# The head of a pooling and state-space decoder step, written in another order

## The chip, the cores and the metric

The kernel runs on one core of a Trainium2 chip. The metric is the device time of one launch in microseconds (us): the median over repeated runs. One further execution is recorded by the hardware profiler. Its span runs from the first instruction to the last; its own time is a little longer. A core has a matrix engine (TensorE, PE in the profile, with PEld for its weight loads), VectorE (DVE), ScalarE (ACT), GpSimd (POOL) and SyncE (SP), which here only issues transfers (DMA).

## The reference

One layer of a decoder, on a prompt of 1,024 rows and on 64 sample rows (8 sequences of 8), model width 1,024. Cut to what the change touches:

```python
mod = jax.nn.silu(c) @ w_ada + b_ada
shift, scale, gate = jnp.split(mod, 3, axis=-1)
h = rmsnorm(x, norm_g) * (1 + scale[:, None]) + shift[:, None]
proj = h @ w_in
u_pool, z_pool, z_ssm, xbc, dt_raw, g_raw = jnp.split(proj, SPLITS, axis=-1)
...
dt = jax.nn.softplus(dt_raw.astype(jnp.float32) + dt_bias.astype(jnp.float32))
...
y = (y + d_skip.astype(jnp.float32)[:, None] * xs).reshape(b, L, D_INNER)
...
gates = jax.nn.sigmoid(g_raw)
m = gates[..., :D_MODEL] * p + gates[..., D_MODEL:] * s
x = x + gate[:, None] * (m @ w_o)
```

Everything behind `proj` (pooling, convolution, the state-space scan, the output projections, the final norm) follows the head and is the same in both kernels.

## The kernel before

All 1,088 rows are kept transposed: a tile has 128 channels on the partitions and 1,088 rows along its free axis, and the model width makes eight such tiles, numbered k. Matrix products in float32 are made from a high and a low part: a matrix is split into `whi` (ACT rounds it) and `wlo` (the rest, by GpSimd or DVE), and the other operand likewise, so each product is three matmuls.

The head is `first()` (L775 to L911) with the lines ahead of it (L127 to L149). It calls `in_line` (L295) at its beginning and end: every instruction that it issues on PE, ACT, DVE, GpSimd and SP keeps the order in which the Python code writes it, engine by engine. Behind the head a scheduler chooses the order. So an instruction that waits holds up all that is written behind it on its engine, and the change is a change of these written orders.

The stages of the head, as written before:

1. `c` (nine rows: one of the prompt, eight of the samples) is loaded into `c9`, ACT takes its silu (L137), PE turns it (transposes it by a matmul with the identity, L142) and DVE copies the result to `scT` (L143). Small vectors in `vb` (among them b_ada and the norm gains) are turned into `vT` (L146 to L148).
2. The rows of x, nine tiles of up to 128 rows: `x_square` (sum of squares, DVE or ACT), `x_root` (ACT), `x_unit` (DVE: reciprocal and scaling in place).
3. `x_turn(g, k)` (L210) turns three groups of rows (x0 and x1; x2 to x4; x5 to x8) for each of the eight k into the tiles `tf[k]`; PE writes a PSUM bank, ACT (odd k) or DVE (even k) copies it out.
4. `ada_mm(part, k)` (L235) multiplies scT by w_ada, eight steps of four matmuls for each of the two parts; `ada_end(part)` (L242) turns the result and adds the bias into `md`. Part 0 serves k = 0 to 3, part 1 serves k = 4 to 7.
5. `h_make(block, ks)` (L264) makes h = tf x scale + shift in high and low parts on ACT and DVE for a block of rows (256, 384 or 448).
6. `products(block, ks)` (L793) multiplies h with two tiles of w_in columns (those of the first gates), six PSUM banks that are filled over k = 0 to 7. `done(block, t)` (L810) takes the sigmoid on ACT and stores it.
7. `late_loads` (L327): its first step issues loads, its second (`next(late)`) copies d_skip into `dx` on DVE (L337), turns `va` (L339) and `dx` (L340) on PE and copies them to `cvT` and `Dv` (L341, L342).
8. `dt_block` (L673): the 32 columns of dt, 32 matmuls for each block.
9. The first pair of column tiles is multiplied by a scheme with seven products instead of eight (`strassen`, L556, with `early=True`). `pair_w.first_steps` (L499) makes its seven split weights from b11, b12, b21 and b22: its first step splits b11 and b21 and forms three differences, later steps split the others. `combine()` (L435) makes the sums S2, S3 and S1 of the tf tiles in place on DVE, ACT copies the high part (L441), DVE makes the low part (L442). The seven products run in `run(wz, hook)`; `hook` interleaves further sums and weight steps.

The low parts and the DVE operations of step 9 share DVE; ACT holds one set of function tables at a time, and each change of set (square root, silu, sigmoid) is an ACT_TABLE_LOAD.

Of the kernel before, what the change touches and what calls it, by code (L numbers as in the profile page):

```python
# [8 lines left out]
F32 = mybir.dt.float32  # L9
F32R = mybir.dt.float32r  # L10
AF = mybir.ActivationFunctionType
ALU = mybir.AluOpType
# [8 lines left out]
P = 128  # L21
D = 1024
KT = D // P
# [23 lines left out]
def tile_pool_ssd_step(  # L47
# [6 lines left out]
    nc = tc.nc  # L54
# [41 lines left out]
    def PB():  # L96
        return psB.tile([P, 512], F32, tag="ps", name=nm("ps"))
# [10 lines left out]
    act = nc.scalar.activation  # L108
    V = nc.vector
# [14 lines left out]
        nc.gpsimd.memset(rc[:, t:t + 1], 1.0 / (t + 1))  # L124


    act(rc[:, 0:1], eps, AF.Silu)  # L127
    nc.gpsimd.memset(rc[:, 0:1], 1.0)
    c9 = R([NB + 1, D])
    store_(c9[0:1, :], c_prompt)  # L130
    store_(c9[1:NB + 1, :], c_sample)
# [2 lines left out]
    store_(vb[16:24, :], norm_g[0].rearrange("(m p) -> m p", p=P))  # L134
    store_(vb[24:40, :], ssm_norm_g[0].rearrange("(m p) -> m p", p=P))
    store_(vb[40:44, :], pool_scale[0].rearrange("(m p) -> m p", p=P))
    act(c9, c9, AF.Silu)  # L137
    scT = const([P, KT, 32], "scT")
    nc.gpsimd.memset(scT, 0.0)
    ps = PB()  # L140
    for k in range(KT):
        nc.tensor.transpose(ps[:, k * 9:k * 9 + 9], c9[:, k * P:(k + 1) * P], ident[:9, :9])  # L142
    V.tensor_copy(scT[:, :, 0:9], ps[:, :72].rearrange("p (k b) -> p k b", b=9))  # L143
    vT = const([P, 44], "vT")
    ps = PB()
    nc.tensor.transpose(ps[:, :44], vb, ident[:44, :44])  # L146
    V.tensor_copy(vT, ps[:, :44])
    V.tensor_scalar(vT[:, 8:16], vT[:, 8:16], 1.0, None, ALU.add)  # L148
    pscl = vT[:, 40:44]  # L149


    def split(raw, kept=None, ncols=P, eng=None):
# [37 lines left out]
    def x_square(i, eng):  # L190
        xt, n = xr[i]
        sqj = pa.tile([P, D], F32, tag="rawA", name=nm("sqj"), bufs=3)
        if eng is V:
            V.scalar_tensor_tensor(sqj[:n], xt[:n], 1.0, xt[:n], ALU.mult, ALU.mult, accum_out=ss[:n, i:i + 1])
        else:
            act(sqj[:n], xt[:n], AF.Square, accum_out=ss[:n, i:i + 1])

    def x_root(a, b):
        n = xr[a][1]
        act(rs[:n, a:b], ss[:n, a:b], AF.Sqrt, bias=eps[:n], scale=1.0 / D)  # L200
# [6 lines left out]

    tf = [None] * KT

    def x_turn(g3, k):  # L210
        if g3 == 0:
            tf[k] = tfp.tile([P, T], F32, tag="tf", name=nm("tf"), bufs=8)
        px = PB()
        c = 0
        for i in range((0, *XG)[g3], XG[g3]):
            xt, n = xr[i]
            nc.tensor.transpose(px[:, c:c + n], xt[:n, k * P:(k + 1) * P], ident[:n, :n])
            c += n
        o = BLK[g3][0]
        if k % 2:  # L220
            act(tf[k][:, o:o + c], px[:, :c], AF.Copy)
        else:
            V.tensor_copy(tf[k][:, o:o + c], px[:, :c])
# [211 lines left out]
    def combine():  # L435
        L_, R_ = slice(0, HF), slice(HF, T)

        big = []

        def parts(src, hi, lo):  # L440
            act(hi, src, AF.Copy)  # L441
            V.tensor_tensor(lo, src, hi.bitcast(F32), ALU.subtract)  # L442

        def part(lst, k, src):
            if lst is S1:
                lst[k] = (hs.tile([P, 2, HF], F32R, tag="sq", name="S1", bufs=1) if k == 3 else R((P, 2, HF), F32R))
            else:
                if k == 0:
                    big.append(Y4(hs).rearrange("p k (j n) -> p k j n", j=2))
                lst[k] = big[-1][:, k]  # L450
            parts(src, lst[k][:, 0], lst[k][:, 1])
        for k in range(4):
            a, b = tf[k], tf[k + 4]
            V.tensor_tensor(b[:, R_], a[:, R_], b[:, R_], ALU.add)
            V.tensor_tensor(a[:, R_], a[:, L_], a[:, R_], ALU.subtract)
            V.tensor_tensor(a[:, L_], b[:, R_], a[:, L_], ALU.subtract)
            part(S2, k, a[:, L_])
            yield
        for k in range(4):
            part(S3, k, tf[k][:, R_])  # L460
        yield
        for k in range(4):
            a, b = tf[k], tf[k + 4]
            V.tensor_tensor(b[:, L_], b[:, L_], a[:, L_], ALU.subtract)
            part(S1, k, b[:, R_])
            if k % 2:
                yield
        for k in range(4):
            parts(tf[k + 4][:, L_], hh_[k][:, R_], hl_[k][:, R_])
            if k % 2:  # L470
                yield
# [303 lines left out]
    def first():  # L775
        ET = mybir.EngineType
        every = (ET.PE, ET.Activation, ET.DVE, ET.Pool, ET.SP)
        in_line(every, True)
        raws = {}

        def w_load(t, j):
            raws[t, j] = raw_()
            c = C_G + D + t * P
            load(raws[t, j], w_in[0, j * 512:(j + 1) * 512, c:c + P].rearrange("(k p) c -> p k c", p=P))

        w = {}

        def w_split(t, j, eng=None):
            w[t, j] = split(raws[t, j], eng=eng)

        banks = {}

        def products(bi, ks):  # L793
            o, n = BLK[bi]
            for t in range(2):
                if (bi, t) not in banks:
                    banks[bi, t] = (PB if (bi, t) in ((1, 1), (2, 0), (2, 1)) else PA)()[:, :n]
            for k in ks:
                for t in range(2):
                    ps = banks[bi, t]  # L800
                    hi, lo = w[t, k // 4]
                    a, b = hi[:, k % 4, :], lo[:, k % 4, :]
                    rh, rl = hh_[k][:, o:o + n], hl_[k][:, o:o + n]
                    mm(ps, a, rh, start=(k == 0), stop=False)
                    mm(ps, b, rh, start=False, stop=False)
                    mm(ps, a, rl, start=False, stop=(k == KT - 1))

        tags = iter(("s1", "u2", "u3", "c2", "s1", "u2"))

        def done(bi, t):  # L810
            o, n = BLK[bi]
            buf = pa.tile([P, HF], F32, tag=next(tags), name=nm("g0"))
            act(buf[:, :n], banks[bi, t], AF.Sigmoid)
            store_(gs_d[t][:, o:o + n], buf[:, :n])

        for i in range(9):
            x_load(i)
        for k in range(KT):
            if k == KT - 2:
                w_load(0, 0)  # L820
                w_load(1, 0)
            ada_load(0, k)
        for k in range(KT):
            if k == 2:
                w_load(0, 1)
                w_load(1, 1)
            ada_load(1, k)
        late = late_loads()
        next(late)

        x_square(0, V)
        x_square(1, V)
        x_root(0, 2)
        x_square(2, None)
        x_unit(0, 2)
        x_square(3, V)
        x_root(2, 4)
        x_square(4, None)
        x_root(4, 5)
        x_unit(2, 4)  # L840
        for k in range(8):
            x_turn(0, k)
        x_unit(4, 5)
        x_square(5, None)
        x_square(7, V)
        x_square(6, None)
        ada_mm(0, 0)
        for k in range(4):
            x_turn(1, k)
        x_root(5, 8)  # L850
        x_unit(5, 8)
        ada_mm(0, 1)
        x_square(8, None)
        x_root(8, 9)
        for k in range(4, 8):
            x_turn(1, k)
        x_unit(8, 9)
        ada_mm(0, 2)
        ada_mm(0, 3)
        for k in range(4):  # L860
            x_turn(2, k)
        ada_mm(0, 4)
        for k in range(4, 8):
            x_turn(2, k)
        ada_mm(0, 5)
        w_split(0, 0)
        w_split(1, 0)
        ada_mm(0, 6)
        ada_mm(0, 7)
        ada_end(0)  # L870

        h_make(0, range(4))
        products(0, range(4))
        h_make(1, range(4))
        ada_mm(1, 0)
        ada_mm(1, 1)
        w_split(0, 1, V)
        w_split(1, 1, V)
        products(1, range(4))
        h_make(2, range(4))  # L880
        for k in range(2, 8):
            ada_mm(1, k)
        products(2, range(2))
        ada_end(1)
        dtw = dt_w()
        products(2, range(2, 4))

        for bi in range(3):
            h_make(bi, range(4, 8))
        next(late, None)  # L890
        for bi in range(3):
            products(bi, range(4, 8))
            for t in range(2):
                done(bi, t)

        run, (wz, wst) = light[0][1], light[0][0]()
        next(wst)
        sums = combine()
        for i in range(3):
            next(sums)  # L900
            dt_block(dtw, i)
        next(sums)
        next(wst)

        def hook(n):
            if 0 < n < 4:
                next(wst)
            if n < 5:
                next(sums)
        run(wz, hook)  # L910
        in_line(every)  # L911
# [950 lines left out]
```

## Time and profile before

| | us |
|---|---|
| median of 3 runs | 1326.1 |
| lowest and highest run | 1325.13, 1326.57 |
| the profiled execution's own time | 1323.45 |
| its span | 1321.4 |
| PE busy in the span | 1264.8 (96%) |
| DVE, ACT, POOL busy | 890.4, 697.6, 679.5 |

A row of a timeline gives start, duration, engine, line, operation, tile written <- tiles read, shapes, count; the bracket tells how long the engine was idle before it and what released it. A row of the stretches gives the length, then busy us and instructions of each engine, the clock granted to PE (1.00 is full), the busy share of the DMA engines and GB/s.

### The profile page before, as it was taken

The numbers are of one execution on the slowest core, as the hardware profiler recorded it, in microseconds if no ns is written. First come the engines' busy times: TensorE is split into PE (matmuls) and PEld (weight loads), VectorE is DVE, ScalarE is ACT, GpSimd is POOL, SyncE is SP. The second block draws the span as 40 slices with busy tenths as digits, with TensorE's granted clock in tenths as the row PEclk, the third lists the DMA queues.
The fourth block names the chain that finished last, engine by engine and source line by source line (L and its number), as shares of the span: only waits on it lengthen the run. The fifth ranks groups of instructions, "written<-read, shape, count | busy, mean of one in ns | idle before, by whom it ended". The sixth has DMA issues, their size and how long they took to land.

```text
span 1321.4 us, 26075 instructions
## 1 busy us (share of the span) xinstructions
PE 1264.8 (96%) x9575; PEld 1164.8 (88%) x9575; DVE 890.4 (67%) x1510; ACT 697.6 (53%) x1661; POOL 679.5 (51%) x564
## 2 busy tenths in 40 slices
PE   5588999999999999999999999999999999999998
PEld 3468989999999999999889999988888888999786
DVE  5647557997967997877657665387565877567433
ACT  4725445656656655555554563667887767201211
POOL 0002666887887787764444453366676646314000
PEclk9898999999999999999999999999999999999999
DMA  9425644554554564543556555999988665475621
GB/s 320 146 68 178 211 167 143 172 178 139 195 192 153 164 188 132 165 149 113 158 143 196 176 159 171 341 346 369 311 268 284 193 202 157 163 262 167 218 100 60
DMA packets 232568, 251.66 MB, mean 190 GB/s; under 512 B 31101, under 2 KB 173573, under 8 KB 232434
## 3 DMA queue, kind: packets, MB, share of 16 engines
q1 hardware_dynamic: 160308, 171.56, 40.9%
q10 hardware_dynamic: 72134, 78.45, 17.4%
q8 instruction: 76, 1.25, 0.4%
q14 instruction: 50, 0.41, 0.1%
HBM read 167.06 MB, written 83.01 MB: 189 GB/s over the span
## 4 chain that ended last, share of the span: by engine, by line
PE 70%; DMA 10%; issue 7%; DVE 5%; POOL 4%; ACT 3%; ACTq 0%; SPq 0%; POOLq 0%; DVEq 0%
PE ps L550 7%; PE mm L550 7%; PE ps L551 7%; PE ps L552 7%; PE mm L552 7%; PE mm L551 7%; PE mm L315 3%; PE mm L316 3%; PE mm L317 3%; PE ps L1810 2%; PE ps L1809 2%; PE ps L1808 2%; PE ps L1134 2%; PE ps L1350 1%; POOL G L1717 1%
## 5 line engine op out<-in xcount | busy, mean ns | idle before, releaser
L158 POOL TENSOR_TENSOR wlo<-rawA,whi 128x512 fp32r<-128x512 f32 x120 | 193.3, 1616 | 198.6 <-ACT whi L155 110.6
L158 POOL TENSOR_TENSOR wlo<-raw,whi 128x512 fp32r<-128x512 f32 x92 | 150.7, 1645 | 131.7 <-ACT whi L155 125.2
L315 PE MATMUL mm<-Y,whi 128*128 128x352 f32 (+1 forms) x480 | 164.8, 343 | 0.8 <-DVE G L1711 0.6
L316 PE MATMUL mm<-Y,whi 128*128 128x352 f32 (+1 forms) x480 | 158.6, 330 | 1.0 <-DVE Y L1385 1.0
L317 PE MATMUL mm<-Y,wlo 128*128 128x352 f32 (+1 forms) x480 | 158.2, 330 | 0.0
L550 PE MATMUL mm<-Y,whi 128*128 128x272 f32 x496 | 146.8, 296 | 1.5 <-ACT dts L683 1.2
L552 PE MATMUL mm<-Y,wlo 128*128 128x272 f32 x496 | 143.1, 289 | 2.5 <-POOL wlo L158 2.5
L550 PE MATMUL ps<-Y,whi 128*128 128x272 f32 x496 | 144.5, 291 | 0.4 <-ACT s L593 0.4
L551 PE MATMUL mm<-Y,whi 128*128 128x272 f32 x496 | 143.2, 289 | 0.4 <-DVE Y L442 0.4
L551 PE MATMUL ps<-Y,whi 128*128 128x272 f32 x496 | 143.1, 289 | 0.0
L552 PE MATMUL ps<-Y,wlo 128*128 128x272 f32 x496 | 142.8, 288 | 0.0
L155 ACT ACTIVATE whi<-rawA 128x512 fp32r<-128x512 f32 x125 | 78.2, 626 | 104.4 <-PE ps L551 46.5
L942 DVE SCALAR_TENSOR_TENSOR GA<-GA,cvT,GA 128x1112 f32<-128x1112 f32 x72 | 130.1, 1812 | 0.0
L155 ACT ACTIVATE whi<-raw 128x512 fp32r<-128x512 f32 x96 | 58.7, 626 | 87.2 <-DVE raw L497 51.5
L550 PEld LDWEIGHTS mm<-Y,whi 128*128 128x128 f32 x496 | 93.4, 188 | 5.9 <-ACT dts L683 2.0
L315 PEld LDWEIGHTS mm<-Y,whi 128*128 128x128 f32 x480 | 91.3, 190 | 6.9 <-issue 4.1
L552 PEld LDWEIGHTS mm<-Y,wlo 128*128 128x128 f32 x496 | 93.4, 188 | 3.5 <-POOL wlo L158 3.2
L550 PEld LDWEIGHTS ps<-Y,whi 128*128 128x128 f32 x496 | 93.3, 188 | 3.4 <-issue 2.7
L551 PEld LDWEIGHTS mm<-Y,whi 128*128 128x128 f32 x496 | 93.4, 188 | 1.5 <-DVE Y L442 0.8
L551 PEld LDWEIGHTS ps<-Y,whi 128*128 128x128 f32 x496 | 93.3, 188 | 0.3 <-issue 0.2
L552 PEld LDWEIGHTS ps<-Y,wlo 128*128 128x128 f32 x496 | 93.4, 188 | 0.2 <-issue 0.2
L316 PEld LDWEIGHTS mm<-Y,whi 128*128 128x128 f32 x480 | 91.4, 190 | 1.7 <-DVE Y L1385 1.6
(446 smaller groups left out, 3784.3 us busy)
## 6 DMA issues: line engine op xcount, KB each, us to landing
rawA<-in_w_in SPq DMA_DIRECT2D x46, 512.0 KB
dec<-acs_d SPq DMA_DIRECT2D x32, 512.0 KB
xbc<-GA ACTq DMA_DIRECT2D x24, 512.0 KB
xb<-xbc SPq DMA_DIRECT2D x32, 384.0 KB
rawA<-in_w_in SPq DMA_DIRECT2D x32, 256.0 KB
pw<-in_w_ssm_out ACTq DMA_DIRECT2D x32, 256.0 KB
ws<-ph ACTq DMA_DIRECT2D x32, 256.0 KB
ws<-pw SPq DMA_DIRECT2D x32, 256.0 KB
```

The lines of the kernel that those rows point to most:

```text
L155: ins = act(hi[:, :, :ncols], raw[:, :, :ncols], AF.Copy)
L158: (eng or nc.gpsimd).tensor_tensor(lo[:, :, :ncols], raw[:, :, :ncols], hi[:, :, :ncols].bitcast(F32), ALU.subtract)
L315: mm(ps[:, :n], a, rh[k][:, o:o + n], start=(k == 0), stop=False)
L316: mm(ps[:, :n], a, rl[k][:, o:o + n], start=False, stop=False)
L317: mm(ps[:, :n], b, rh[k][:, o:o + n], start=False, stop=(k == nk - 1))
L550: mm(p, hi, ah, start=(k == 0), stop=False)
L551: mm(p, hi, al, start=False, stop=False)
L552: mm(p, lo, ah, start=False, stop=(k == 3))
L942: V.scalar_tensor_tensor(d[:, :n], rp[:, k:k + n], cvT[:, 24 * k + mc:24 * k + mc + 1], d[:, :n], ALU.mult, ALU.add)
L1134: mm(o[hh], xd[:S, 2 * q + hh, :], dec[:S, 2 * q + hh], start=True, stop=state is None)
L1808: mm(ps[:, :cw], mhk, wo[k][0][:, s], start=(k == 0), stop=False)
L1809: mm(ps[:, :cw], mhk, wo[k][1][:, s], start=False, stop=False)
```

## The change

The written order of the head is rearranged; the operations are the same apart from the engine of one square and two copies.

- The silu of `c` moves from the start into the turning of the third row group (`c_turn`), and so does the turning of `vb` (`v_turn`). ACT's first table load is that of the square root.
- The roots and scalings of x stand earlier, one square moves from DVE to ACT, and the first four turnings are all copied by DVE. The ada steps of part 0 stand together behind the third group's first four turnings; the turnings (2, 5) to (2, 7) stand behind the first `h_make`.
- In `combine`, the low part of each S2 tile is written behind the next tile's sums.
- `next(late)` moves from ahead of the second half's products to behind the last sigmoids and the first sums. The next pair's first weight step (`next(wst)`) moves ahead of the sigmoids, the first sums ahead of the last two sigmoids.

```diff
-    act(rc[:, 0:1], eps, AF.Silu)
-    nc.gpsimd.memset(rc[:, 0:1], 1.0)
...
-    act(c9, c9, AF.Silu)
+
+    act(rc[:, 0:1], eps, AF.Sqrt)
+    nc.gpsimd.memset(rc[:, 0:1], 1.0)
...
+    def c_turn():
+        act(c9, c9, AF.Silu)
+        ps = PB()
+        for k in range(KT):
+            nc.tensor.transpose(ps[:, k * 9:k * 9 + 9], c9[:, k * P:(k + 1) * P], ident[:9, :9])
+        V.tensor_copy(scT[:, :, 0:9], ps[:, :72].rearrange("p (k b) -> p k b", b=9))
+
+    def v_turn():
+        ps = PB()
+        nc.tensor.transpose(ps[:, :44], vb, ident[:44, :44])
+        V.tensor_copy(vT, ps[:, :44])
+        V.tensor_scalar(vT[:, 8:16], vT[:, 8:16], 1.0, None, ALU.add)
...
+        def low(k):
+            V.tensor_tensor(S2[k][:, 1], tf[k][:, L_], S2[k][:, 0].bitcast(F32), ALU.subtract)
         for k in range(4):
             a, b = tf[k], tf[k + 4]
+            room(S2, k)
             V.tensor_tensor(b[:, R_], a[:, R_], b[:, R_], ALU.add)
             V.tensor_tensor(a[:, R_], a[:, L_], a[:, R_], ALU.subtract)
             V.tensor_tensor(a[:, L_], b[:, R_], a[:, L_], ALU.subtract)
-            part(S2, k, a[:, L_])
-            yield
+            act(S2[k][:, 0], a[:, L_], AF.Copy)
+            if k:
+                low(k - 1)
+            if k < 3:
+                yield
+        low(3)
+        yield
...
         x_root(0, 2)
+        x_unit(0, 2)
         x_square(2, None)
-        x_unit(0, 2)
-        x_square(3, V)
+        x_square(3, None)
         x_root(2, 4)
+        for k in range(4):
+            x_turn(0, k, V)
+        x_unit(2, 4)
         x_square(4, None)
         x_root(4, 5)
-        x_unit(2, 4)
-        for k in range(8):
+        for k in range(4, 8):
             x_turn(0, k)
         x_unit(4, 5)
         x_square(5, None)
         x_square(7, V)
         x_square(6, None)
-        ada_mm(0, 0)
+        x_root(5, 8)
         for k in range(4):
             x_turn(1, k)
-        x_root(5, 8)
         x_unit(5, 8)
-        ada_mm(0, 1)
         x_square(8, None)
         x_root(8, 9)
         for k in range(4, 8):
             x_turn(1, k)
         x_unit(8, 9)
-        ada_mm(0, 2)
-        ada_mm(0, 3)
+        v_turn()
+        for k in range(2):
+            x_turn(2, k)
+        c_turn()
+        for k in range(2, 4):
+            x_turn(2, k)
         for k in range(4):
-            x_turn(2, k)
-        ada_mm(0, 4)
-        for k in range(4, 8):
-            x_turn(2, k)
-        ada_mm(0, 5)
+            ada_mm(0, k)
         w_split(0, 0)
         w_split(1, 0)
-        ada_mm(0, 6)
-        ada_mm(0, 7)
+        for k in range(4, 8):
+            ada_mm(0, k)
+        x_turn(2, 4)
         ada_end(0)
 
         h_make(0, range(4))
+        for k in range(5, 8):
+            x_turn(2, k)
         products(0, range(4))
...
-        next(late, None)
         for bi in range(3):
             products(bi, range(4, 8))
+
+        run, (wz, wst) = light[0][1], light[0][0]()
+        next(wst)
+        for bi in range(2):
             for t in range(2):
                 done(bi, t)
-
-        run, (wz, wst) = light[0][1], light[0][0]()
-        next(wst)
         sums = combine()
+        next(sums)
+        for t in range(2):
+            done(2, t)
+        next(late, None)
         for i in range(3):
+            dt_block(dtw, i)
             next(sums)
-            dt_block(dtw, i)
-        next(sums)
         next(wst)
```

More of the change, by code (lines that the diff above doesn't have):

```diff
@@ L208, in tile_pool_ssd_step, with x_turn @@
     tf = [None] * KT
-    def x_turn(g3, k):
+    def x_turn(g3, k, eng=None):
         if g3 == 0:
@@ L219, in x_turn @@
         o = BLK[g3][0]
-        if k % 2:
+        if eng is not V and k % 2:
             act(tf[k][:, o:o + c], px[:, :c], AF.Copy)
@@ L442, in parts, with room @@
             V.tensor_tensor(lo, src, hi.bitcast(F32), ALU.subtract)
-        def part(lst, k, src):
+        def room(lst, k):
             if lst is S1:
@@ L450, in part @@
                 lst[k] = big[-1][:, k]
+        def part(lst, k, src):
+            room(lst, k)
             parts(src, lst[k][:, 0], lst[k][:, 1])
+        def low(k):
+            V.tensor_tensor(S2[k][:, 1], tf[k][:, L_], S2[k][:, 0].bitcast(F32), ALU.subtract)
         for k in range(4):
             a, b = tf[k], tf[k + 4]
+            room(S2, k)
             V.tensor_tensor(b[:, R_], a[:, R_], b[:, R_], ALU.add)
```

8 lines of the change are left out of this document (removed).

## The prediction

> **What bounds the kernel now.** I read the page first, then the busy time of each engine in stretches of 10 us, then the timeline of each engine up to the stretch where TensorE (PE) is full.
>
> ```profile
> span 1321.4 us, 26075 instructions
> PE 1264.8 (96%) x9575; PEld 1164.8 (88%) x9575; DVE 890.4 (67%) x1510; ACT 697.6 (53%) x1661; POOL 679.5 (51%) x564
> ```
>
> ```profile
> core 0: us, PE busy (x) PEld busy (x) DVE busy (x) ACT busy (x) POOL busy (x), PEclk, DMA share, GB/s
> 0.00:10.00 10.00, 0.99 (x8) 0.92 (x8) 2.83 (x7) 4.49 (x6) 2.66 (x31) 1.00 0.82 289
> 10.00:20.00 10.00, 5.96 (x29) 4.08 (x30) 7.64 (x18) 5.68 (x14) 0.00 (x0) 1.00 1.03 327
> 20.00:30.00 10.00, 9.61 (x73) 6.29 (x71) 6.36 (x12) 4.56 (x10) 0.00 (x0) 1.00 1.08 370
> ...
> 60.00:70.00 10.00, 2.83 (x13) 2.80 (x14) 6.71 (x21) 5.84 (x9) 0.00 (x0) 0.50 0.00 1
> ...
> 120.00:130.00 10.00, 10.00 (x82) 10.00 (x81) 5.52 (x12) 4.71 (x11) 7.47 (x6) 1.00 1.03 361
> sum 130.00, PE 94.85 PEld 77.28 DVE 77.67 ACT 66.82 POOL 13.91; mean PE 7.30 PEld 5.94 DVE 5.97 ACT 5.14 POOL 1.07
> ```
>
> PE is idle 1321.4 - 1264.8 = 56.6 us in all, and 130.0 - 94.85 = 35.2 us of that lie in the first 130 us, the head that the change rewrites. Behind it PE bounds the kernel, so what the head ends earlier, the whole ends earlier, as long as transfers and weights keep up. Within the head the engines take turns: in 60 to 70 PE has 2.83 us of work while DVE and ACT make h, and afterwards DVE waits while PE multiplies. That alternation is the largest single loss, and these rows show its cause:
>
> ```profile
> 55.51 0.27 PE L339 MATMUL ps<-ident,va 120*128 120x120 f32 x1
> 67.17 0.28 PE L340 MATMUL ps<-ident,dx 16*128 16x16 f32 x1 [11.39 <-DVE dx L337]
> ...
> 81.09 0.37 PE L806 MATMUL ps<-G,whi 128*128 128x448 f32 x1
> 81.39 1.07 PE L680 MATMUL mm<-Y,dtw 128*32 128x256 f32 x16
> ...
> 87.22 1.69 PE L680 MATMUL mm<-G,dtw 128*32 128x448 f32 x16
> ```
>
> ```profile
> 66.36 0.63 DVE L270 TENSOR_TENSOR G<-tf,G 128x448 fp32r<-128x448 f32 x1 [0.38 <-ACT G L287]
> 66.91 0.21 DVE L337 COPY dx<-dk 16x128 f32<-16x128 f32 x1
> ...
> 83.50 1.29 DVE L158 TENSOR_TENSOR wlo<-rawA,whi 128x512 fp32r<-128x512 f32 x2 [15.64 <-ACT whi L155]
> ```
>
> PE waits 11.39 us for a 0.21 us copy of d_skip that stands on DVE behind all of h. The second half's products then run alone to 81.46, ACT takes the six sigmoids, and only then come the next pair's splits: DVE idles 15.64 us.
>
> **Part 1, d_skip turned later, weights ahead of the last sigmoids: +16.5 us.** The products of k = 4 to 7 follow h tile by tile, and ACT splits b11 and b21 straight behind its last h operation, ahead of the sigmoids' table load. DVE can then start its splits when its last h operation ends, 66.36 + 0.63 = 67.0, instead of at 83.50: 16.5 us on the old time base. The products took 67.45 to 81.46, 14.0 us with a half-clock start (0.50 in 60 to 70), so some 12 at full clock; h takes 53.87 (row in part 3) to 67.0, which is room enough, and only the last six of 72, about 1.2 us, come after h. The two buffers that the splits take were freed by the first half's products, which end at 55.5. The six sigmoids and stores now lie beside DVE's work, which I cost at nothing; without that cover the last two alone, with the split behind them, cost the 2.0 us from 81.46 to 83.50. No DMA is added; on SP's queue only one pair of loads changes places, much later.
>
> **Part 2, rows, turning and silu: +0.7 us.**
>
> ```profile
> 6.97 1.06 ACT L137 ACTIVATE R<-R 9x1024 f32<-9x1024 f32 x1 [4.08 <-DMA R<-in_c_sample]
> 8.04 1.28 ACT L200 ACT_TABLE_LOAD   x1
> 9.33 0.29 ACT L200 ACTIVATE rs<-ss,eps 128x2 f32<-128x2 f32 x1
> ```
>
> ```profile
> 8.12 0.99 PE L142 MATMUL ps<-ident,R 9*128 9x9 f32 x8 [8.12 <-ACT R L137]
> ...
> 18.20 1.08 PE L239 MATMUL ps<-Y,scT 128*32 128x256 f32 x8 [2.16 <-DVE sqj L194]
> ...
> 22.98 2.04 PE L217 MATMUL ps<-ident,Y 128*128 128x128 f32 x12
> 24.95 1.07 PE L239 MATMUL ps<-Y,scT 128*32 128x256 f32 x16
> ```
>
> ```profile
> 7.21 0.08 DVE L194 DVE_READ_ACCUMULATOR sqj<-Y 128x1 f32 x1
> ...
> 26.10 0.75 DVE L206 TENSOR_SCALAR R<-R,rs 64x1024 f32<-64x1024 f32 x1
> ...
> 35.15 1.06 DVE L254 TENSOR_TENSOR md<-md,vT 128x36 f32<-128x36 f32 x1
> 36.13 0.18 DVE L251 TENSOR_TENSOR md<-ps,vT 128x36 f32<-128x36 f32 x1
> ```
>
> The root waits no more for silu and its table change: 7.3 instead of 9.33. The second group's turning no longer stands behind the first ada product (18.20). Stepping through the new order with these durations, x8 is normalised at about 21 instead of 26.85. But now silu stands in the middle: a table load of 1.28 and 1.06 of silu behind ACT's copy of turning (2,1), so from about 22.9 to 25.3, and behind it wait ACT's next copy, the splits of the first weights, and on PE the turning of c (0.99), the rest of group 2 and all eight ada products. scT is ready at 26.8, and after two more turnings ada starts at about 28. Its weights have landed by then: x, ada part 0 and two weight tiles are 9.17 MB, and 289, 327 and 370 GB/s bring 9.86 MB in 30 us.
>
> One ada step takes 0.53 us at 24.95 (16 records in 1.07), but 1.08 at 18.20 (8 in 1.08): PE ran at half pace early, although the clock column says 1.00 there. In the new order PE idles some 3 us for silu. All eight fast end at 32.2, all slow at 37.1. Behind them come one turning (four transposes of 0.17, as at 22.98: 0.7), the rest of its copy, which DVE has ahead of md (0.3), and the transposes and md themselves, about 0.95 (from 52.88 until just before h at 53.87 the second time, rows in part 3, which leaves no room for a step like the 1.06 at 35.15). That is md at 34.15 or 39.05, against 36.13 + 0.18 = 36.31. Unbroken PE work turned the pace between 18.20 and 24.95 before; I let it turn after some 4 us of work, near 29.7, one or two slow steps: md at 35.6, +0.7 (bounds -2.7 and +2.2).
>
> [...]
>
> **Part 3, the stretch from md to the second md: +1.6 us.**
>
> ```profile
> 37.00 0.39 PE L804 MATMUL mm<-Y,whi 128*128 128x256 f32 x1 [2.12 <-ACT Y L278]
> ...
> 42.26 1.07 PE L239 MATMUL ps<-G,scT 128*32 128x256 f32 x16
> ...
> 52.88 0.38 PE L247 MATMUL ps<-ident,mr 128*128 128x128 f32 x2
> ```
>
> ```profile
> 38.94 1.22 DVE L270 TENSOR_TENSOR Y<-tf,Y 128x256 fp32r<-128x256 f32 x3
> ```
>
> ```profile
> 53.87 1.10 ACT L278 ACTIVATE G<-tf,md 128x256 fp32r<-128x256 f32 x2 [2.99 <-DVE md L251]
> ...
> 100.42 0.61 ACT L155 ACTIVATE whi<-rawA 128x512 fp32r<-128x512 f32 x1
> ```
>
> The first 24 products take 37.00 to 42.26, 5.3 us after an idle 2.12; 24 of 272 columns take 2.99 in part 4, so these of 256 ran near half pace. With three turnings now filling that gap, they end about 0.5 after the last low part (40.16), so near 40.6 on the old base: 1.6 earlier, and PE is unbroken from there to 52.88. The three postponed copies, two on ACT and one on DVE, each about the 0.61 us of ACT's 128x512 copy at 100.42, delay the second block's h by some 1 us, which its lead over PE holds. Parts 2 and 3 give 2.3 (from -1.1 to +3.8), so DVE's splits start at 67.0 - 2.3 = 64.7; I call this D.
>
> **Part 4, from D to the last product of the early pair: -0.3 us.**
>
> ```profile
> 88.28 0.73 DVE L456 TENSOR_TENSOR tf<-tf,tf 128x544 f32<-128x544 f32 x1
> 89.73 0.72 DVE L442 TENSOR_TENSOR Y<-tf,Y 128x544 fp32r<-128x544 f32 x1 [0.72 <-ACT Y L441]
> ```
>
> ```profile
> 101.09 0.60 PE L550 MATMUL mm<-G,whi 128*128 128x272 f32 x1 [3.96 <-ACT whi L155]
> ...
> 106.60 0.28 PE L550 MATMUL mm<-Y,whi 128*128 128x272 f32 x1
> ...
> 112.58 0.29 PE L550 MATMUL mm<-R,whi 128*128 128x272 f32 x1
> ...
> 117.24 0.29 PE L550 MATMUL mm<-Y,whi 128*128 128x272 f32 x1
> ```
>
> Before, the third product waited for weights (whi at 100.42) behind four sums on DVE, each of which stood 0.72 us for ACT's copy. Putting the low part behind the next sums saves three of these, 2.2 us; dx, cvT and Dv take about 1.0 of it back. DVE's chain is thus 1.2 us shorter, but it no longer decides. The stall goes here: PE ends the products near D + 1.2 and now waits for dx behind DVE's first sums, which end 5.5 after D (from 83.50 to 88.28 + 0.73 = 89.01). dt_block starts at D + 6.05 and takes 81.39 to 88.91 = 7.5; on ACT the dt copies and on SP the next pair's first weight tile, which waits for dt's buffer, are queued behind it, all still earlier than before. Six products of 2.99 (106.60 to 112.58 is two) reach D + 31.5. After an idle 3.96 us the product at 101.09 ran 5.51 instead of 2.99, 2.5 us lost; PE idles as long before dt_block, so I charge 2.5 again: the seventh product starts at D + 34.05, before it was 117.24 - 83.50 = 33.74. Bounds: +2.2 if the pace holds, -2.5 if it stays low twice as long.
>
> **Sum.** 16.5 + 0.7 + 1.6 - 0.3 = 18.5 us. The profiled execution took 1323.45 us (span 1321.4 and 2.05 around it), so 1305.0; the median of the runs shown, 1326.1, is 2.65 above it: 1307.6. All bounds good: 16.5 + 3.8 + 2.2 = 22.5, 1303.6. All bad: 16.5 - 1.1 - 2.5 = 12.9, 1313.2.
>
> **Rivals.**
> [...]
> - Warm throughout: 1303.6. [...]
> - The next pair takes part of it back: DMA share is 1.03 from 120 to 130, and the weights behind the early pair come late. For it: that share; against it: the loads wait for buffers, which come free earlier by the same shift. At half the gain, 1316.8; at all of it no change, 1326.
> - Slower: the half pace sticks. PE stands between DVE's sums from dt_block on, and if small waits there keep the clock low until the early pair's last product, 7.5 + 7 x 2.99 = 28.4 us of work take 28.4 more, 25.9 beyond what I charged: 1307.6 + 25.9 = 1333.5. It decides once 18.5 + 2.5 = 21.0 us of that work run slow. Stretch 60 to 80 shows a long slow spell; against it, by 106 the pace was full again.
>
> **How the numbers follow.** Forecast 0.68, cold 0.13, warm 0.05, half back 0.07, all back 0.03, slower 0.04. Forecast, cold and warm lie within 1303.6 to 1313.2; the medians' spread (1325.13 to 1326.57) widens this to 1302.5 to 1315.0, with 0.14 left out. A measurement of this kernel tells some 0.2%, 2.7 us, from no change: faster 0.93, same 0.03, slower 0.04.
>
> **What would show it.** Right: no PE wait over 1 us for dx before the second half's products, which end about 1 us after the last h; the splits of rawA on DVE at 63 to 68; dt_block near 71; the stretch after 110 at 10 of 10. Wrong in part 2: md later than 37.5, or ada at 1.08 a step throughout. Wrong in part 4: clock at 0.50 for over 7 us after dt_block begins. The forecast falls if the rawA splits start later than 72, or if PE's idle time after the head grows by over 5 us.

## The result, and the profile after

| | before | after |
|---|---|---|
| median, us (4 runs each) | 1325.62 | 1306.71 |
| lowest and highest run | 1322.3, 1326.57 | 1303.54, 1307.45 |
| ratio of the medians, 95% interval | | 0.9857 [0.9833, 0.9881] |
| the profiled execution's own time | 1323.45 | 1307.45 |

The changed kernel is 18.9 us faster by the medians and 16.0 us by the two profiled executions. The forecast was 1307.6 for the median, 1305.0 for the profiled execution. The page of the changed kernel:

```profile
span 1305.4 us, 26075 instructions
PE 1261.2 (97%) x9575; PEld 1159.5 (89%) x9575; DVE 899.9 (69%) x1510; ACT 698.7 (54%) x1661; POOL 677.9 (52%) x564
```

The instruction counts are those of before. PE's idle time fell from 56.6 us to 1305.4 - 1261.2 = 44.2. The stretches of 10 us of the same execution (length, busy us and count of each engine, granted clock, DMA share, GB/s) say where:

```profile
20.00:30.00 10.00, 5.57 (x35) 3.50 (x38) 3.36 (x9) 3.91 (x6) 0.00 (x0) 0.62 1.08 369
...
60.00:70.00 10.00, 7.96 (x41) 7.32 (x41) 9.16 (x23) 7.36 (x13) 0.00 (x0) 1.00 0.05 16
70.00:80.00 10.00, 8.06 (x77) 3.30 (x81) 9.35 (x17) 4.03 (x8) 0.00 (x0) 0.66 0.31 113
...
110.00:120.00 10.00, 10.00 (x82) 10.00 (x81) 1.83 (x2) 3.21 (x7) 7.66 (x7) 1.00 0.97 348
...
sum 130.00, PE 106.13 PEld 85.54 DVE 85.09 ACT 75.40 POOL 25.68; mean PE 8.16 PEld 6.58 DVE 6.55 ACT 5.80 POOL 1.98
```

The head's first 130 us now hold 130.0 - 106.13 = 23.9 us of idle PE, against 35.2: 11.3 of the 12.4 us. In 60 to 70 PE has 7.96 us of work where it had 2.83, beside 9.16 on DVE. In exchange 20 to 30 lost: 5.57 instead of 9.61, at a clock of 0.62. Three timelines carry the reading; first PE's:

```profile
25.66 1.02 PE L147 MATMUL ps<-ident,R 9*128 9x9 f32 x8 [2.99 <-ACT R L144]
...
28.87 5.53 PE L244 MATMUL ps<-Y,scT 128*32 128x256 f32 x64
...
67.63 0.36 PE L823 MATMUL ps<-G,whi 128*128 128x448 f32 x1
67.83 0.27 PE L344 MATMUL ps<-ident,va 120*128 120x120 f32 x1
71.94 0.28 PE L345 MATMUL ps<-ident,dx 16*128 16x16 f32 x1 [3.85 <-DVE dx L342]
72.16 1.94 PE L697 MATMUL mm<-Y,dtw 128*32 128x256 f32 x16
...
82.02 0.39 PE L567 MATMUL mm<-Y,whi 128*128 128x272 f32 x1
...
99.01 0.39 PE L568 MATMUL mm<-S,whi 128*128 128x272 f32 x1 [0.44 <-DVE S L447]
100.86 0.29 PE L567 MATMUL mm<-Y,whi 128*128 128x272 f32 x1
```

Then DVE's and ACT's:

```profile
35.99 0.19 DVE L256 TENSOR_TENSOR md<-ps,vT 128x36 f32<-128x36 f32 x1
...
65.73 0.62 DVE L275 TENSOR_TENSOR G<-tf,G 128x448 fp32r<-128x448 f32 x1 [0.39 <-ACT G L292]
66.27 1.29 DVE L163 TENSOR_TENSOR wlo<-rawA,whi 128x512 fp32r<-128x512 f32 x2
...
71.68 0.21 DVE L342 COPY dx<-dk 16x128 f32<-16x128 f32 x1
...
80.83 0.73 DVE L462 TENSOR_TENSOR Y<-tf,Y 128x544 fp32r<-128x544 f32 x1 [0.47 <-ACT Y L469]
83.90 0.73 DVE L462 TENSOR_TENSOR Y<-tf,Y 128x544 fp32r<-128x544 f32 x1 [2.34 <-ACT Y L469]
...
98.24 0.72 DVE L447 TENSOR_TENSOR S<-tf,S 128x544 fp32r<-128x544 f32 x1
```

```profile
65.60 1.14 ACT L160 ACTIVATE whi<-rawA 128x512 fp32r<-128x512 f32 x2
66.75 1.28 ACT L830 ACT_TABLE_LOAD   x1
...
82.17 0.64 ACT L700 ACTIVATE dts<-mm,dtb 128x448 f32<-128x448 f32 x1 [1.36 <-PE mm L697]
...
83.20 0.66 ACT L469 ACTIVATE Y<-tf 128x544 fp32r<-128x544 f32 x1 [0.40 <-ACT dts L700]
```

The wait of 11.39 us and the one of 15.64 us are gone. The second half's products end at 68.0 beside h, ACT's split of b11 and b21 at 65.60 stands ahead of the table load, and DVE's splits follow h without a gap: D, the start of `wlo<-rawA`, moves from 83.50 to 66.27, 17.2 us. What is left is a new, shorter loop: PE waits 3.85 us for dx at 71.94 and then runs dt_block slowly (sixteen matmuls in 1.94 us at 72.16), ACT's dt copy waits for PE (82.17), and DVE waits 2.34 us for the ACT copy behind that one (83.90).

Six marks follow the head through all kernels below: md (end of the second md operation, here 35.99 + 0.19 = 36.18), the second md, D, the start of dt_block, S (start of the last low part, `S<-tf,S`, here 98.24), and the seventh product of the early pair. The kernel before, PE's timeline where it takes S:

```profile
115.39 0.40 PE L551 MATMUL mm<-S,whi 128*128 128x272 f32 x1 [0.62 <-DVE S L442]
```

PE waits for DVE there, 0.62 us; at 99.01 in the changed kernel it waits 0.44.

### The profile page after: what moved, and what is told of

Read it like the earlier page. It is cut to its first block, busy times and chain, and to the rows that moved or that the text cites. A ratio compares the mean times of both kernels' runs of the same rounds, so it can differ in the third digit from the quotient of the medians.

```text
span 1305.4 us, 26075 instructions
## 1 busy us (share of the span) xinstructions
PE 1261.2 (97%) x9575; PEld 1159.5 (89%) x9575; DVE 899.9 (69%) x1510; ACT 698.7 (54%) x1661; POOL 677.9 (52%) x564
## 4 chain that ended last, share of the span: by engine, by line
PE 48%; DVE 4%; DMA 4%; POOL 3%; issue 3%; ACT 3%; ACTq 0%; SPq 0%; POOLq 0%; DVEq 0%
PE mm L320 4%; PE mm L321 4%; PE mm L322 4%; PE ps L567 3%; PE ps L568 3%; PE ps L569 3%; PE mm L567 3%; PE mm L569 3%; PE mm L568 3%; PE ps L1831 2%; PE ps L1833 2%; PE ps L1832 2%; PE ps L1157 2%; PE ps L1373 1%; PE ps L1160 1%
## 5 line engine op out<-in xcount | busy, mean ns | idle before, releaser
L160 ACT ACTIVATE whi<-raw 128x512 fp32r<-128x512 f32 x96 | 58.8, 626 | 92.4 <-DVE raw L514 58.2
```

What stands on the lines that cost most here:

```text
L160: ins = act(hi[:, :, :ncols], raw[:, :, :ncols], AF.Copy)
```

## The experiments

Each kernel was timed in five rounds beside the kernel before; the table gives the ratio to it with its interval, the difference in us (the ratio's distance from 1, times 1325), and the marks of its one profiled execution. The kernel before had medians of 1323.1, 1322.8 and 1326.7 in the three groups (each group on a chip of its own), so only ratios are compared across groups. An interval reaches 2.5 to 3.7 us to either side. The changed kernel, with 0.9857 and 0.9844, stands at -19 to -21; gains and losses below are counted from the mean of the two, -19.8. Behind S, where nothing was edited, the fourteen profiled executions take between 1202.0 us (i_part1_undone) and 1208.8 us (d_low_back) to the end of the span. A difference of a few us in time need not come from the head, so the marks are read beside the times.

| kernel | ratio [95%] | us | md | D | dt_block | S |
|---|---|---|---|---|---|---|
| before | 1 | 0 | 36.3 | 83.5 | 81.4 | 114.6 |
| after | 0.9857 [0.9833, 0.9881] | -18.9 | 36.2 | 66.3 | 72.2 | 98.2 |
| a_late_back | 0.9917 [0.9895, 0.9938] | -11.0 | 35.0 | 66.0 | 80.2 | 103.9 |
| b_weights_back | 0.9908 [0.9882, 0.9935] | -12.2 | 37.5 | 74.5 | 80.4 | 106.6 |
| c_rows_back | 0.9888 [0.9866, 0.9910] | -14.8 | 36.5 | 68.4 | 74.3 | 99.6 |
| d_low_back | 0.9890 [0.9867, 0.9913] | -14.6 | 37.5 | 67.6 | 74.9 | 101.4 |
| e_part1_only | 0.9882 [0.9854, 0.9909] | -15.6 | 37.0 | 69.0 | 76.3 | 102.5 |
| f_silu_gap | 0.9822 [0.9798, 0.9846] | -23.6 | 33.2 | 63.3 | 69.2 | 95.2 |
| g_dx_early | 0.9824 [0.9800, 0.9848] | -23.3 | 36.9 | 67.0 | 69.2 | 95.1 |
| h_both | 0.9794 [0.9769, 0.9818] | -27.3 | 33.6 | 63.7 | 65.9 | 91.9 |
| after_again | 0.9844 [0.9824, 0.9863] | -20.7 | 34.7 | 64.8 | 70.6 | 96.0 |
| i_part1_undone | 0.9939 [0.9919, 0.9959] | -8.1 | 35.4 | 81.4 | 79.3 | 109.4 |
| j_only_late | 0.9927 [0.9908, 0.9946] | -9.7 | 37.0 | 74.2 | 81.6 | 108.1 |
| k_dx_early_low_back | 0.9856 [0.9830, 0.9883] | -19.1 | 38.0 | 68.1 | 70.4 | 99.8 |

### One part of the change undone at a time

**d_skip's turning back in front of the second half's products.**

```diff
         for bi in range(3):
             h_make(bi, range(4, 8))
+        next(late, None)
         for bi in range(3):
             products(bi, range(4, 8))
...
-        next(late, None)
         for i in range(3):
             dt_block(dtw, i)
```

> The changed kernel with one step put back: the turning of d_skip and the convolution's vectors stands again ahead of the second half's products. Theory 1 (what PE waits for sets the end of the head: products, then dt_block): ACT and DVE still reach the next pair's splits at 66.3 us, but the products start only when DVE's last h operation has ended, at about 66.9 instead of beside h, and end near 80, so dt_block starts at about 80 instead of 72.2. 8 us slower than the changed kernel, about 1315. Rival (DVE's chain of splits and sums sets it, and the place of the weights does it all): within 1.5 us of the changed kernel.

Some 8.8 us of the gain are lost, as expected. PE's timeline of this kernel, then DVE's:

```profile
65.35 0.28 PE L345 MATMUL ps<-ident,dx 16*128 16x16 f32 x1 [11.39 <-DVE dx L342]
...
80.20 1.07 PE L697 MATMUL mm<-Y,dtw 128*32 128x256 f32 x16
```

```profile
65.95 1.28 DVE L163 TENSOR_TENSOR wlo<-rawA,whi 128x512 fp32r<-128x512 f32 x2
...
77.46 0.73 DVE L462 TENSOR_TENSOR Y<-tf,Y 128x544 fp32r<-128x544 f32 x1 [3.87 <-ACT Y L469]
```

The stall of before is back to the hundredth (11.39), and dt_block starts at 80.20, yet DVE's splits still start at 65.95. DVE doesn't keep that lead. ACT's sigmoids wait for the late products, ACT's copies of S2 stand behind the sigmoids and the dt copies, and DVE waits for those copies: 3.87 us at 77.46, then 3.51 and 2.16. S comes 5.6 us later than in the changed kernel, less than the 8.0 of dt_block.

**The next pair's first weights and the first sums back behind the sigmoids.**

```diff
             products(bi, range(4, 8))
+            for t in range(2):
+                done(bi, t)
 
         run, (wz, wst) = light[0][1], light[0][0]()
         next(wst)
-        for bi in range(2):
-            for t in range(2):
-                done(bi, t)
         sums = combine()
         next(sums)
-        for t in range(2):
-            done(2, t)
         next(late, None)
```

> The changed kernel with the other half of part 1 put back: the next pair's first splits and the first sums stand again behind all six sigmoids; d_skip stays behind the first sums. Theory 1: ACT takes the sigmoids from 66.9 to about 72 and only then splits, so DVE's chain and with it dx and dt_block start 6 us later: about 1312.5. Rival (PE has enough other work there, the sigmoids are hidden): within 1.5 us of the changed kernel.

Some 7.6 us are lost. ACT's and DVE's timelines of this kernel:

```profile
67.05 1.28 ACT L830 ACT_TABLE_LOAD   x1
...
73.85 1.15 ACT L160 ACTIVATE whi<-rawA 128x512 fp32r<-128x512 f32 x2 [0.46 <-ACT g L830]
```

```profile
74.52 1.29 DVE L163 TENSOR_TENSOR wlo<-rawA,whi 128x512 fp32r<-128x512 f32 x2 [6.82 <-ACT whi L160]
```

The table load and six sigmoids with their stores take ACT from 67.05 to 73.85, and DVE stands idle for those 6.82 us. Undoing either of the two moves alone thus costs about 8 us.

**The front (rows, turnings, silu, ada) back in the order of before**; everything from the second `h_make` on as changed. The core of the edit, besides silu and the turnings of c and vb going back to the start and the first two ada steps going ahead of and amid the second group's turnings:

```diff
...
-        v_turn()
-        for k in range(2):
-            x_turn(2, k)
-        c_turn()
-        for k in range(2, 4):
-            x_turn(2, k)
-        for k in range(4):
-            ada_mm(0, k)
+        ada_mm(0, 2)
+        ada_mm(0, 3)
+        for k in range(4):
+            x_turn(2, k)
+        ada_mm(0, 4)
+        for k in range(4, 8):
+            x_turn(2, k)
+        ada_mm(0, 5)
         w_split(0, 0)
         w_split(1, 0)
-        for k in range(4, 8):
-            ada_mm(0, k)
-        x_turn(2, 4)
+        ada_mm(0, 6)
+        ada_mm(0, 7)
         ada_end(0)
 
         h_make(0, range(4))
-        for k in range(5, 8):
-            x_turn(2, k)
```

> The changed kernel with the old order of everything up to the first h (silu at the start, rows, turning, ada steps). The prediction says 2.3 us slower, about 1309. What the changed kernel's trace shows (DVE's splits start at 66.27 instead of 67.0 with the old front) says 0.7 us slower, about 1307.4.

The loss is about 5 us by the ratio, more than expected, though its interval overlaps with one of the changed kernel's two. In the trace md stands at 36.45, as in the changed kernel, but from md to D are 31.96 us against 30.09 (e_part1_only, with the same front, has 32.02, and the seven executions with the new front in which DVE's splits follow h at once and the products lie beside it have 30.08 to 30.10). These 1.9 us lie between md and the second md, and they aren't fixed. The other two executions with the old front, of the kernel before and of j_only_late, lose far less there: from md to the second md they take 17.52 and 17.25, c_rows_back and e_part1_only 18.87 and 18.91, the changed kernel 16.99. The granted clock differs in the same way. Behind md it is at 0.50 for 3.4 us in the first two (37.73 to 41.15 and 37.84 to 41.25), for 6.8 us in the other two (37.49 to 44.31 and 38.09 to 44.92), and with the new front not at all. So the front is worth 0.3 to 1.9 us behind md, and the other 3 aren't placed.

**The low parts of S2 back behind each copy.**

```diff
-            act(S2[k][:, 0], a[:, L_], AF.Copy)
-            if k:
-                low(k - 1)
-            if k < 3:
-                yield
-        low(3)
-        yield
+            part(S2, k, a[:, L_])
+            yield
```

> The changed kernel with the low part of each S2 tile again right behind its own ACT copy. The prediction (DVE's chain is not what decides there, PE is): within 0.5 us of the changed kernel, 1306.7. Rival (DVE's chain decides up to the sixth product): the three waits of 0.72 us come back, 2.2 us slower, 1308.9.

About 5 us are lost; the interval, like that of c_rows_back, overlaps with one of the changed kernel's two. The trace shows too that the claim that this edit doesn't decide is wrong. DVE's timeline of this kernel:

```profile
73.79 0.72 DVE L447 TENSOR_TENSOR Y<-tf,Y 128x544 fp32r<-128x544 f32 x1 [0.72 <-ACT Y L446]
74.43 0.21 DVE L342 COPY dx<-dk 16x128 f32<-16x128 f32 x1
...
80.13 0.73 DVE L447 TENSOR_TENSOR Y<-tf,Y 128x544 fp32r<-128x544 f32 x1 [2.60 <-ACT Y L446]
83.73 0.72 DVE L447 TENSOR_TENSOR Y<-tf,Y 128x544 fp32r<-128x544 f32 x1 [0.72 <-ACT Y L446]
```

The first low part now stands ahead of dx, with its wait of 0.72: dx starts 74.43 - 67.57 = 6.86 us after D instead of 71.68 - 66.27 = 5.41, and PE waits for dx. The later low parts wait again (2.60, then 0.72 each). From D to S are 33.82 us against 31.97, 1.85 more, although PE needs less from dt_block's start to the first product here (9.1 us, against 9.86). D is 1.3 later, by md alone, which is scatter; what remains of the 5 us lies within the intervals.

### Part 1 alone, and part 1 undone

**Both of the last two together** (old front, old low parts): part 1 alone on the kernel before.

> The kernel before with part 1 alone: d_skip later, the next pair's weights and first sums ahead of the last sigmoids; rows, silu, turning and the low parts as before. Prediction: 16.5 us of the gain is here, less the 0.3 of part 4 and without the low parts' saving, so 1309.5 to 1310.5. Rival (the front of the head carries most of it): over 1315.

It came out as expected: -15.6 us, interval -19 to -12, where the prediction's part 1 had 16.5. In its one profiled execution D comes 14.5 us earlier than before and S 12.1.

**d_skip and weights both back**: part 1 undone, the front and the low parts as changed.

> The changed kernel with both halves of part 1 put back at once (d_skip ahead of the second half's products; splits and sums behind the sigmoids); the rows, silu, turning and low parts of the change stay. Theory 1: part 1 carries all but about 2 us, so this lies 1 to 3 us below the kernel before, and what both halves cost together (14 to 17 us) is more than the sum of what each cost alone, since each of them alone still lets the other run ahead. Rival (the rest of the change carries a third or more): over 6 us below the kernel before.

Still 8.1 us faster than before, more than the theory allowed (1 to 3); the rival, over 6, came true. DVE's timeline of this kernel:

```profile
81.41 1.30 DVE L163 TENSOR_TENSOR wlo<-rawA,whi 128x512 fp32r<-128x512 f32 x2 [15.04 <-ACT whi L160]
...
109.44 0.72 DVE L447 TENSOR_TENSOR S<-tf,S 128x544 fp32r<-128x544 f32 x1
```

The long idle of DVE is back (15.04), but from D to S are 28.03 us, against 31.11 before: the low parts alone give 3.1 here. Before, DVE waited four times for a copy of S2 (0.72, 0.72, 0.73 and 0.72 us, ahead of 89.73, 93.34, 96.95 and 100.55); here it waits for none of the four. D itself is 2.1 earlier. That makes 5.2 at S; the time's interval is 5.4 to 10.7. The parts overlap: 15.6 + 8.1 = 23.7, together they give 19 to 21. Undoing both halves of part 1 costs 11.7, less than the 8.8 + 7.6 of each alone, and not more as the theory had it.

**Only d_skip and dt_block moved**, in the kernel before: the sigmoids stay ahead of the weights.

```diff
-        next(late, None)
         for bi in range(3):
             products(bi, range(4, 8))
...
         sums = combine()
+        next(sums)
+        next(late, None)
         for i in range(3):
-            next(sums)
             dt_block(dtw, i)
-        next(sums)
+            next(sums)
```

> The kernel before with one step alone: the turning of d_skip behind the first sums; the splits and sums stay behind the sigmoids, everything else as before. Theory 1: the products run beside h, the splits start near 74 instead of 83.5: 8 to 11 us faster than before. Rival (the place of the weights is what counts): under 4 us faster.

-9.7 us, as expected. The wait for d_skip has only moved, as PE's timeline shows:

```profile
81.36 0.28 PE L341 MATMUL ps<-ident,dx 16*128 16x16 f32 x1 [12.19 <-DVE dx L338]
81.57 1.94 PE L685 MATMUL mm<-Y,dtw 128*32 128x256 f32 x16
```

PE waits longer than before (12.19) and dt_block starts no earlier (81.57), but the products now lie beside h, so ACT's sigmoids and DVE's splits come 9.3 us earlier (D at 74.22). PE's waiting time is not what was gained; DVE's start is.

### Taking away what the change newly made late

**Silu out of the turnings**, ahead of the third group's first two:

```diff
     def c_turn():
-        act(c9, c9, AF.Silu)
         ps = PB()
...
         v_turn()
+        act(c9, c9, AF.Silu)
         for k in range(2):
             x_turn(2, k)
         c_turn()
```

> The changed kernel with silu of c (and its table load) written ahead of the third group's first two turnings, where ACT idles from 19.9 to 22.7, instead of behind them. Theory 2 (part 2 won so little because silu stood in front of PE: PE idle 2.99 us, then half clock from 22.5 to 32.7): PE goes on, ada is bounded by its weights, md comes 2.5 to 4.5 us earlier, 1302.5 to 1304.5. Rival (the weights of ada or the stretch behind set md anyway): within 1 us of the changed kernel.

-23.6 us, 3.8 better than the changed kernel, though the intervals overlap. PE's timeline of this kernel:

```profile
22.91 1.02 PE L146 MATMUL ps<-ident,R 9*128 9x9 f32 x8
...
26.11 5.31 PE L243 MATMUL ps<-Y,scT 128*32 128x256 f32 x64
```

The wait of 2.99 us for silu is gone and ada starts at 26.11 instead of 28.87. The low clock is not gone (0.50 from 19.28 to 29.52), and the 64 ada matmuls take 5.31 us. md ends at 33.21, about 3 earlier, and below all eight executions that have silu where the change put it (34.72 to 38.04).

**dx early, its turning behind dt_block**:

```diff
         V.tensor_copy(dx, dk.unsqueeze(2).to_broadcast([16, 2, 64]))
+        yield
         ps = PB()
...
         next(wst)
+        next(late, None)
         for bi in range(2):
...
-        next(late, None)
         for i in range(3):
             dt_block(dtw, i)
             next(sums)
+        next(late, None)
         next(wst)
```

> The changed kernel with the copy of d_skip on DVE in front of the first sums and its turning on PE behind dt_block, so that PE waits for nothing between the products and dt_block. Theory 3 (part 4: the wait moved to dx, and with it the half clock, hold PE and through the dt copies also ACT and DVE): dt_block starts at about 68.5 instead of 72.2 at full clock, then DVE's chain decides, 2.5 to 3.5 us faster, about 1303.7. Rival (DVE's chain already decides): within 1 us.

-23.3 us, 3.5 better, again with overlapping intervals. PE's timeline of this kernel, then DVE's:

```profile
69.21 1.07 PE L698 MATMUL mm<-Y,dtw 128*32 128x256 f32 x16 [0.50 <-ACT g L831]
70.09 1.05 PE L698 MATMUL mm<-G,dtw 128*32 128x256 f32 x16
...
77.07 0.40 PE L568 MATMUL mm<-Y,whi 128*128 128x272 f32 x1
```

```profile
95.14 0.72 DVE L448 TENSOR_TENSOR S<-tf,S 128x544 fp32r<-128x544 f32 x1
```

dt_block starts 2.2 us after D and runs at full clock (sixteen matmuls in 1.05 to 1.07, against 1.94 in the changed kernel). The first product starts 10.1 us after D instead of 15.75, 5.7 earlier, but S only 3.8 earlier (28.15 against 31.97). Now DVE's own work decides: from D to 86.56 it has no wait.

**Both of these**:

> Silu in ACT's gap and the copy of d_skip early, both together. If both theories hold the gains add up: 5 to 8 us faster than the changed kernel, 1299 to 1302.

The gains add up: -27.3 us, 1296.83 us where the kernel before had 1322.79, with an interval just below both of the changed kernel's. This is the fastest version found.

**dx early, with the low parts of before**:

> The copy of d_skip early, as in g_dx_early, but with the low part of each S2 tile again right behind its ACT copy. With PE held up no more by dx, theory 3 says that DVE's chain decides: the three waits of 0.72 us come back in full, 2.2 us slower than g_dx_early, against 0.976 of before that is about 0.984 of the kernel before less what dx gave. Rival (PE still decides): within 0.5 us of g_dx_early.

-19.1 us, 4.2 behind g_dx_early, with overlapping intervals; from D to S 31.61 us against 28.15. With PE no longer held by dx, the stalls of the low parts reach S in full: 3.5 us, more than the 1.85 of d_low_back. DVE waits four times here (0.72, 1.12, 0.72 and 0.72); the expectation counted three waits, 2.2 us.

**The changed kernel once more**, unedited:

> The changed kernel itself, as the measure for the kernels of this batch and for the earlier batches, whose runs of the kernel before lay 2.5 to 2.8 us lower than in the first comparison. All theories: 0.986 of the kernel before.

1304.82 us, 0.9844. Its marks show the spread of one program: md 34.72 (36.18 in the first execution), D to S 31.19 (31.97).

## Why the prediction was right, and where it was not

The time, its sign and the likeliest case came out. By the profiled executions 1305.0 was predicted and 1307.45 measured; the 2.45 us split by the marks.

- **Part 1 (16.5): the mechanism is right; the size is met in time, not at the marks.** Alone it measures 15.6 in time, interval 12 to 19. The two profiled executions differ by 14.9, of which S shows 12.1; the other 2.8 lie behind S, where nothing was edited. All its steps show: the products in the shadow of h, the last of them ending 1.7 us after D (1.2 predicted), the split ahead of the table load, no wait over 1 us ahead of the second half's products. What the prediction did not see is how the two moves share it: each undone alone loses about 8.
- **Part 2 (0.7): nothing is left of it.** md came at 36.18 instead of 35.6. In the eight executions with the new front as changed, md lies between 34.72 and 38.04, on average 36.4; in the four with the old front between 36.31 and 36.97, on average 36.7. The wait for silu was as worked out (2.99 us, ada from 28.87), and the 64 ada matmuls took 5.53, partly slow (the clock at 0.50 until 32.71), as assumed. That the pace turns after some 4 us of work was the author's estimate, and no run shows it: from the start of PE's unbroken work to the end of the low clock it took 7.05 us here (25.66 to 32.71), 5.3 in after_again (25.05 to 30.39) and 8.0 in f_silu_gap (21.49 to 29.52). The term was inside its bounds; the scatter of 3.3 us with one and the same code is what no single value could meet, and it goes with the clock (last section).
- **Part 3 (1.6): the mechanism holds, its size depends on the base.** From md to the second md are 16.99 us in the changed kernel, 17.52 in the execution of before that the sum used (0.5), 17.25 in j_only_late (0.3), and 18.87 and 18.91 in c_rows_back and e_part1_only (1.9). Against its own base the term was three times too large; whether the low clock behind md lasts 3.4 us or 6.8 was not in the sum.
- **Part 4 (-0.3): its terms right, one statement wrong.** dt_block started 5.89 us after D (6.05), and from there to the first product 9.86 us passed instead of 7.5: the 2.5 charged for the half clock. The seventh product started at D + 34.59 (34.05). The step that failed is "DVE's chain is thus 1.2 us shorter, but it no longer decides". It does decide: with the low parts put back S comes 1.85 us later after D, and with dx taken off PE's path 3.5 later. The saving was also counted as three waits, 2.2 us; where nothing else holds ACT, four go (3.1 in i_part1_undone, 3.5 between g_dx_early and k_dx_early_low_back). The missing link is ACT. Its dt copies wait for PE, the S2 copies are queued behind them, and DVE waits for these (2.34 at 83.90). The prediction noted the dt copies as queued but did not follow that queue on to DVE.
- **Behind the head** nothing was given back: from the seventh product to the end of the execution it took 1206.2 us before and 1206.6 after. PE's idle time there was 21.4 and is 44.2 - 23.9 = 20.3 us, and the stretch 110 to 120 is at 10.00 of 10. The rivals of half the gain or all of it returned, and of a half pace that sticks, fall; the clock was low from 70.25 to 77.08, 4.9 us of it after dt_block began.
- **Two slips in the bounds.** Eight slow ada steps of 1.08 from 28 end at 36.6, not 37.1, so part 2's lower bound is -2.2. A pace that stays low twice as long costs 2.5 more than charged, so part 4's is -2.8, not -2.5. The two nearly cancel: 1313.0 with all bounds bad, instead of 1313.2.

The four differences: md 0.58 late, md to D 1.00 longer than predicted, D to the seventh product 0.54, the rest 0.38 (2.50, since 1305.0 is 1304.95 rounded). That the median was met so closely is luck: the profiled executions differ by 16.0 us where 18.5 were forecast, but that of before lay 2.65 below the median used and that of the changed kernel 0.7 above its own.

## What to carry to other kernels

In these runs a wait on an engine was worth what stood behind it on the other engines, not its own length. The 11.39 us on PE held back ACT and, through ACT's order, DVE (15.64 us idle). Moving only the wait (j_only_late), with DVE's start 9 us earlier, paid half (9.7 of 19.8 us). With the wait still in place and DVE's start as early as in the changed kernel (a_late_back), only just over half of the gain was left (11.0 us), because DVE then waited for ACT in the middle of its chain (3.87 us at 77.46). When a stall is moved, follow its queue through every engine until it comes back: PE to ACT to DVE here, and each new place where it stood (silu, dx) was worth another 3 to 4 us (3.8 and 3.5). A single profiled execution is a base with its own luck; where two executions of one program differ by 1.5 us at a mark, a term of that size isn't resolved by one of them.

## What the runs showed of the hardware

The granted clock fell although PE was busy for 40% of the 3.4 us before, and stayed low through 6.8 us (25.88 to 32.71) in which PE was busy throughout. Four stretches of 3.4 us of the changed kernel's first execution, and three around dt_block (same columns as above):

```profile
19.05:22.47 3.42, 1.36 (x8) 0.89 (x8) 3.31 (x9) 0.94 (x3) 0.00 (x0) 1.00 1.05 388
22.47:25.88 3.41, 0.42 (x3) 0.25 (x4) 0.15 (x1) 2.88 (x3) 0.00 (x0) 0.50 1.12 337
25.88:29.30 3.42, 3.42 (x21) 2.27 (x24) 0.86 (x2) 0.33 (x1) 0.00 (x0) 0.50 1.05 384
29.30:32.71 3.41, 3.41 (x37) 1.57 (x33) 0.00 (x0) 1.25 (x3) 2.50 (x2) 0.50 0.65 201
66.84:70.25 3.41, 1.26 (x7) 0.89 (x5) 3.34 (x6) 2.46 (x4) 0.00 (x0) 1.00 0.15 50
70.25:73.67 3.42, 1.73 (x17) 0.97 (x21) 2.95 (x7) 1.91 (x4) 0.00 (x0) 0.50 0.41 149
73.67:77.08 3.41, 3.41 (x32) 1.38 (x28) 3.31 (x6) 1.03 (x3) 0.00 (x0) 0.50 0.36 135
```

After a stretch with 1.36 of 3.42 us busy (40%) the clock is 0.50, and it stays there through two stretches that are busy throughout. After the one at 66.84, with 1.26 of 3.41 (37%), it is 0.50 as well. The same kernel in after_again, in stretches of 3.4 us:

```profile
20.40:23.80 3.40, 0.95 (x5) 0.58 (x5) 1.56 (x4) 1.70 (x2) 0.00 (x0) 0.96 1.07 371
23.80:27.20 3.40, 2.15 (x13) 1.68 (x14) 0.23 (x1) 1.18 (x2) 0.00 (x0) 0.50 1.11 352
27.20:30.60 3.40, 3.40 (x28) 1.72 (x32) 0.62 (x1) 1.58 (x3) 1.10 (x1) 0.53 1.05 378
30.60:34.00 3.40, 3.40 (x52) 1.98 (x45) 0.34 (x1) 0.38 (x1) 1.42 (x2) 1.00 0.69 161
```

Here the low clock begins over 1 us later and ends before 31, and the 64 ada matmuls took 4.69 us instead of 5.53. The low spell begins at another moment in each of these two executions of one program (22.47, and 23.56 in after_again). The spells read here last close to whole multiples of 3.4 us: 3.42 in the kernel before (37.73 to 41.15), 6.83 in after_again (23.56 to 30.39), 10.24 in the changed kernel's first execution (22.47 to 32.71). In the kernel before, the 0.50 of stretch 60 to 70 sets in during an idle time of 11.39 us (0.50 from 58.2); the slow pace at 18.20 follows an idle time of only 2.16 us, with the clock recorded as 1.00, so that row doesn't show a fall of the clock.

Read in stretches of 0.1 us, the low spell ahead of md in the eight executions whose code is the same up to md:

| execution | clock at 0.50 from | to | md |
|---|---|---|---|
| after_again | 23.56 | 30.39 | 34.72 |
| a_late_back | 23.71 | 30.53 | 35.01 |
| i_part1_undone | 21.26 | 31.50 | 35.37 |
| after | 22.47 | 32.71 | 36.18 |
| g_dx_early | 22.96 | 33.20 | 36.89 |
| d_low_back | 20.26 | 33.91 | 37.48 |
| b_weights_back | 20.63 | 34.28 | 37.51 |
| k_dx_early_low_back | 21.01 | 34.66 | 38.04 |

The later the spell ends, the later md comes, in all eight. The spells last 6.8, 10.2 or 13.7 us. At dt_block it is the same: from D to S are 31.97 and 31.85 us where the clock is low for 6.8 us there (after, f_silu_gap), 31.19 and 31.20 where it is low for 3.4 (after_again, c_rows_back). That the clock causes these scatters is argued from this order and not tried: no run moved a spell and left the rest as it was.
